# Moving the reload of the recurrence heads to GpSimd behind all Fourier columns, and spreading 32 modulation steps over 22 rounds

## Chip, cores and metric

The kernel runs on one core of a Trainium2 chip. The metric is the time of one execution on the device, in microseconds (us), as the median of several runs. The engines are named as the profile names them: PE is TensorE (matrix products; PEld is its loading of weights), DVE is VectorE, ACT is ScalarE, POOL is GpSimd, SP is SyncE, which here only issues DMAs.

## What is computed

One layer of a hybrid backbone on 512 latent and 256 context tokens of width 2048, all in float32:

```python
mod_lat = einsum("bd,ldm->lbm", silu(c), w_ada) + b_ada[:, None, :]      # six modulations
h_lat = modulate(rms_norm(x, g[0]), ml[0], ml[1])
y_lat, y_ctx = mixing_sublayer(h_lat, h_ctx, w_in, w_four, conv_w, conv_b, lru_w, lru_b, lru_lam, w_out, ...)
x = x + ml[2] * rms_norm(y_lat, g[1])
f_lat = swiglu(modulate(rms_norm(x, g[2]), ml[3], ml[4]), w_ffn_in, w_ffn_out)
x = x + ml[5] * rms_norm(f_lat, g[3])
```

`mixing_sublayer` multiplies by `w_in` and splits the columns: Fourier groups (a discrete Fourier transform over grid and channels, its real part, then a linear map per group), and recurrent head groups (a convolution, gates, a forward and a backward scan, times a GeLU gate). Both are joined and multiplied by `w_out`. `swiglu` is the channel mixer with 5632 hidden channels.

## The kernel before

**Numbers in pairs.** A float32 operand is split in two parts of a reduced format, a high part (a copy or cast, on ACT or DVE) and a low part (a subtraction, on DVE); each product is three matmuls, high by high, high by low and low by high (`mm3`). In the profile wh and wl are the parts of a weight unit, fh and fl those of a Fourier column unit, mxh and mxl those of a recurrence head.

**The stream of weights.** `Stream` holds a list of units of 512 KB in the order in which the products take them. `use` hands out one unit, and calls `prep` for the units ahead of it (`la` of them); `prep` splits a unit and calls `dma` for those still further ahead (`ra` of them). Each load takes a buffer of the pool raw, in turn, and so waits for the last reader of what lay there before; all loads of the stream are issued by SP, in order.

**Fourier columns** (395 to 490 us). 16 column units of `w_in` (n = 16 to 31 in the list) are folded (fo), split (fh, fl, ext) and multiplied into the banks f and fx. Beside them run the last gates and scans of the recurrence (`lru_step`: the ACT functions sigmoid, exp and square root, the scans on DVE); finished heads are stored to rec_d in DRAM by POOL, and each of four heads is loaded again as a unit of the stream (`rec_unit`) for the output projection. Behind n = 29, 30 and 31 stands one head each, and the last head behind them; `get_rec` takes them. In this stage `open_c` also loads the tables CX, CW, SW (raw<-cw_d), CG and SG by POOL, and splits them (th, thw, tl, tlw).

**Fourier transform and after.** From F, Fx and the tables PE forms y, whose split parts Y feed z, in two passes of 60 matmuls each; the results and the four heads are the inputs of the output projection (oq), from 527 us on.

**Second product of the channel mixer** (1615 to 2111 us). Two halves of the output columns, each of 22 rounds: one unit of activations (act_d) and two of `w_ffn_out`, 48 matmuls into the banks fo. In the first half the last modulation is summed as well: 32 steps (`gstep`), each a load of 512 KB of `w_ada` (gr, by SP, L385) and a multiply-add on DVE (ga<-gr,sil,ga). `tick(KN["Q6"])` behind each round adds Q6 to an account and issues one step for each whole number. After the half, eight matmuls gr turn the two sums ga into rows.

Instructions that one engine gets run in its program order; the order is set by the code and by priorities at build time, and every wait is a semaphore.

Of the kernel before, what the change touches and what calls it, by code (L numbers as in the profile page):

```python
# [17 lines left out]
P = 128  # L18
# [4 lines left out]
NE, NO = 258, 254  # L23
DFF = 5632
EPS = 1e-6
KN = {'p2k': 1, 'lord': 0, 'lag': 3, 'cws': 0, 'xo': 'xNcxxxcx..XX.X...C......X...C.C..C.X...X', 'xd': 3, 'order': 'xxsscxssxxxxxsssccc', 'TL': 3, 'TS': 7, 'Q7': 1.75, 'nA': 8, 'nB': 5, 'nX': 9, 'nO': 7, 'nE': 4, 'laA': 1, 'raA': 6, 'laB': 1, 'raB': 3, 'laO': 1, 'raO': 4, 'Q1': 3, 'Q2': 1.0, 'Q3': 0, 'Q4': 1.0, 'Q5': 2.5, 'Q6': 4.0, 'early': 3, 'tail': 'acb0de1f2', 'steps': 27, 'shift': 1, 'l1': 2000, 'vC': 0.1, 'pA': -100, 'vO': 0.25, 'sq': 2000, 'pO': 30, 'gvC': -2000, 'pX': -100, 'pC': -30, 'gvX': -30, 'xp': 300, 'pG': -800, 'p1': 100, 'tb': -30, 'gp': 2000, 'gvB': -30, 'vF': 0.25, 'hcp': -2000, 'mc': 800, 'rp': -800, 'vA': 0.25, 'gvF': -300, 'T2': 800, 'fs': 300, 'T5': -100, 'gvD': -100, 'op': -30, 'hp': 30, 'ni': 300, 'vB': 0.25, 'ysp': 300, 'T4': 800, 'gvR': 300, 'T1': -30, 'fi': 300, 'gvA': 800, 'T3': -800, 'pD': 800}

C_BADA, C_C, C_NG, C_CW, C_CB, C_LAM, C_LB, C_END = 0, 96, 128, 192, 224, 232, 248, 280

# [62 lines left out]
class Stream:  # L92
# [11 lines left out]
        self.lim = self.ends.popleft()  # L104
        self.prep(self.nu + self.la)

    def add(self, dmas, f):
        self.items.append([dmas, f, None])

    def dma(self, upto):  # L110
        while self.nd < min(upto, self.lim):
            it = self.items[self.nd]
            it[2] = self.alloc([1024], name="raw")
            for dst, src in it[0]:
                self.nc.sync.dma_start(dst(it[2]), src)
            self.nd += 1

    def prep(self, upto):
# [18 lines left out]
def block_kernel(ctx, tc, a, out, dump=None):  # L137
    nc = tc.nc
# [4 lines left out]
    def open_pools(side, *specs):  # L143
        stack = ExitStack()
        for n, names in specs:
            first = names.split()[0]
            cnt[0] += 1
            po = stack.enter_context(tc.tile_pool(name=f"{first}_pool{cnt[0]}", bufs=n, side=side, reuse_waits="tile"))
            for x in names.split():
                pools[x] = po  # L150
        return stack
# [5 lines left out]
    sc = open_pools("left", (8, "x ch clo"))  # L157
    sp_ = open_pools("right", (KN["nA"], RAW), (16 - KN["nA"], WH), (6, "c cT"))
    pst = ExitStack()
# [35 lines left out]
    def prq(key):  # L195
        return tc.high_priority(offset=KN.get(key, 0))

# [10 lines left out]
    def split(src, hi, lo):  # L208
        share[0] += KN.get("v" + S.key, 0)
        on_v = share[0] >= 1  # L210
        share[0] -= on_v
        (V.tensor_copy if on_v or load.even and load.t["A"] > load.t["V"] + 3000 else A.copy)(hi, src)
        V.tensor_tensor(lo, src, f(hi), op=OP.subtract)
# [31 lines left out]
        if not fill:  # L245
            owed[0] = 0.0

# [1 line left out]
    S = Stream(nc, st)  # L249
    S.pr, S.key = prq, "A"  # L250
    act_d = dr.tile([DFF, SEQ], F32, name="act_d")
# [1 line left out]
    rec_d = dr.tile([1024, SEQ], F32, name="rec_d")  # L253
# [5 lines left out]
    def kv(n):  # L259
        return lambda raw: raw.rearrange("p (k c) -> p k c", k=n)  # L260

    def wunit(w, r0, nk, c0, nw, po=("wh", "wl")):
        S.add([(kv(nk), w[r0:r0 + nk * P, c0:c0 + nw].rearrange("(k p) c -> p k c", p=P))], split_to((nk, nw), *po))
# [34 lines left out]
    def first_steps():  # L298
        g = 0
        for s in range(72):  # L300
            yield s, range(g, 64) if s == 71 else range(g, max(g, min(64, s - 7 - KN["lag"])))
            g = max(g, min(64, s - 7 - KN["lag"]))

    for s, go in first_steps():
        if s == KN["cws"]:
            S.add([(lambda raw: raw[:, 0:512].rearrange("p (k c) -> p k c", k=2), a["t_cc"].rearrange("(k p) c -> p k c", p=P))],
# [7 lines left out]
        if s < 64:  # L314
            cb, m, kq = s // 8, s // 4 % 2, s % 4
# [11 lines left out]
    def lru_w(h, d, m):  # L327
        S.add([(lambda raw, g=g: raw[:, g * 256:(g + 1) * 256].rearrange("p (k c) -> p k c", k=2),
                a["lru_w"][d, g, h, :, m * P:(m + 1) * P].rearrange("(k p) c -> p k c", p=P)) for g in range(2)], lru_prep)
# [4 lines left out]
        return hi, lo  # L334

    def rec_unit(h):
        S.add([(kv(2), rec_d[h * 256:(h + 1) * 256, :].rearrange("(k p) c -> p k c", p=P))], mix_prep)

    LRU_STEPS = [min(32, max(0, n - KN["shift"]) * 32 // KN["steps"]) for n in range(33)]
    for n in range(32):  # L340
        for c in range(LRU_STEPS[n], LRU_STEPS[n + 1]):
            if c % 4 < 2:
                lru_w(c // 8, c // 4 % 2, c % 4)
        k = n % 8
        if n < 16:
            wunit(wi, k * 256, 2, 2048 + n // 8 * 512, 512)
        else:
            c0 = (n // 8 - 2) * 512
            S.add([(kv(2), wi[k * 256:(k + 1) * 256, c0:c0 + 512].rearrange("(k p) c -> p k c", p=P))], fold_w)
            if n >= 29:  # L350
                rec_unit(n - 29)
    rec_unit(3)
    OUT = [(2, k) for k in (4, 5, 6, 7, 0, 1, 2, 3)] + [(q, k) for q in (3, 0, 1, 0, 1) for k in range(8)]
    for qd, kq in OUT:
        wunit(wo, kq * 256, 2, qd * 512, 512)
# [19 lines left out]
                wunit(a["w_ffn_out"], k * P, 1, hf * 1024, 1024, po[1 + k % 2])  # L375
    S.end()

# [1 line left out]
    gacc, graw, gmods = {}, {}, [(m, k, h) for m in (3, 4, 2, 5) for h in range(2) for k in range(KT)]  # L379

    def gload(i):
# [39 lines left out]
            T.matmul(b[:, 2 * j:2 * j + 2], acc[:, j * P:(j + 1) * P], ones[:, 0:2], start=j == 0, stop=j == 7, skip_group_check=True)  # L421
        V.tensor_copy(m34[:, m - 3, h * 8:(h + 1) * 8], b[:, 0:16].rearrange("p (j s) -> p j s", s=2)[:, :, 0])

# [1 line left out]
    xt = [[st([1024], name="x") for _ in range(2)] for _ in range(4)]  # L425
    ct = [[st([1024], name="c") for _ in range(2)] for _ in range(2)]
    st1, st2, st3 = st([P], name="stg"), st([P], name="stg"), st([P], name="stg")
# [9 lines left out]
    for z in KN["order"]:  # L437
        if z == "s":
            S.dma(S.nd + 1)
        elif z == "c":  # L440
            t, h = cts.popleft()
            nc.sync.dma_start(ct[t][h], a["ctx"][t * P:(t + 1) * P, h * 1024:(h + 1) * 1024])
        else:
            t, h = xts.popleft()
            nc.sync.dma_start(xt[t][h], a["x"][t * P:(t + 1) * P, h * 1024:(h + 1) * 1024])
    S.phase()
    while cts:
        t, h = cts.popleft()
# [16 lines left out]
    for g in (64, 96):  # L465
        V.tensor_tensor(sel, sel, ident[:, g:g + 2], op=OP.add)

# [1 line left out]
    nstat = [0]  # L469

    def rstd_of(ss, n, scale=1.0):
# [32 lines left out]
    squares(xt, 0)  # L504
    norm_in(xt, 0, 0.5)

# [1 line left out]
    S.la, S.ra = KN["laA"], KN["raA"]  # L508
    @prio("cw")
    def cw_part(row, cs):  # L510
# [26 lines left out]

    cch = ccl = cex = w4 = None

# [1 line left out]
    def xT_bank(tiles, k, o):  # L541
        for t in range(len(tiles)):
            T.transpose(o[:, t * P:(t + 1) * P], tiles[t][k // 8][:, (k % 8) * P:(k % 8 + 1) * P], ident)
# [39 lines left out]
                xT_bank(ct, 4 * kq + 2 * k + j, b[:, n * 512 + j * 256:n * 512 + (j + 1) * 256])  # L583
        A.copy(flat(cT[kq][:, 2 * ks[0]:2 * ks[-1] + 2, :]), b[:, 0:512 * len(ks)])

# [1 line left out]
    mods = cst.tile([P, 4, KT], F32, name="mods")  # L587
    hl, hc = {}, {}

# [111 lines left out]
    S.phase()  # L701
    load.even = False

# [1 line left out]
    lam = cols[:, C_LAM:C_LAM + 16]  # L705
    lt = cst.tile([P, 6, 16], F32, name="lt")
    mx, e, w, w2, acc, spc = (lt[:, i, :] for i in range(6))
# [12 lines left out]
    V.tensor_tensor(acc, acc, mx, op=OP.add)  # L720
    V.tensor_scalar(spc, acc, -8.0, None, op0=OP.mult)

# [1 line left out]
    def unfold(dst, E, O, neg=False):  # L724
        p, m = (OP.subtract, OP.add) if neg else (OP.add, OP.subtract)
        d3 = dst.rearrange("p (r c) -> p r c", c=64)
# [73 lines left out]
    S.key = "G"  # L800
    r_done(1, rb, rc)

# [1 line left out]
    sqrt_ins = []  # L804

    def lru():
# [99 lines left out]
            tick(KN["Q2"])  # L906
        g_done(grp, gb)

# [1 line left out]
    F, mix, tables = [], {}, {}  # L910
    load_c = []

    def get_rec(h):
        r = S.use()
        for m in range(2):
            mix[8 + 2 * h + m] = [tuple(x[:, m, t * P:(t + 1) * P] for x in r) for t in range(4)]
# [20 lines left out]
    for hf in range(2):  # L937
        fb = bank("f")
        for kq in range(8):
            lru_step(16 + 8 * hf + kq)  # L940
            hi, lo, ex = S.use()
            for k in range(2):
                kt = 2 * kq + k
                h = hl[kt]
                for g in range(2):
                    for e, sl in ((0, slice(0, NE)), (1, slice(NE, 512))):
                        mm3(fb[:, g * 512:(g + 1) * 512][:, sl], (hi[:, k, g, e, :], lo[:, k, g, e, :]), (h[0][:, sl], h[1][:, sl]),
                            kt == 0 and e == 0, kt == 15)
                for n in range(2):
                    T.matmul(fxb[:, 0:NE], ex[:, k, :], h[n][:, 0:NE], start=hf + kt + n == 0, stop=hf * kt * n == 15)  # L950
            if hf and kq == 4:
                open_c()
            if hf and kq > 4:
                get_rec(kq - 5)
            tick(KN["Q3"])
        for g in range(2):
            t = st([2, 512], F32R, "F")
            with prq("fs"):
                split(fb[:, g * 512:(g + 1) * 512], t[:, 0, :], t[:, 1, :])
            F.append(t)  # L960
# [2 lines left out]
    Fx = st([2, 258], F32R, "Fx")  # L963
    with prq("fs"):
        split(fxb[0:8, 0:NE], Fx[0:8, 0, :], Fx[0:8, 1, :])
    get_rec(3)

# [1 line left out]
    CX, CW, SW, CG, SG = (tables[n] for n in ("CX", "CW", "SW", "CG", "SG"))  # L969
    for pr in range(2):  # L970
        Y = []
# [41 lines left out]
            mix[c] = [(t[:, 0, i * P:(i + 1) * P], t[:, 1, i * P:(i + 1) * P]) for i in range(4)]  # L1013
    del Y, CW, SW, CX, CG, SG, F, Fx, tables

# [1 line left out]
    def out_kts(bankof, kq, ts, start, stop):  # L1017
        hi, lo = S.use()
        for t in ts:
# [27 lines left out]

    S.key = "D"

# [1 line left out]
    xr, hv, hq = {}, {}, {}  # L1051

    def p0(t):
# [71 lines left out]
                V.tensor_tensor(y[t][1], y[t][1], G2[1], op=OP.mult)  # L1125
    mix.clear()

    # ---- channel mixer, first product: seven products of half blocks (Strassen, Winograd's form), halves of gate
    # and up channels, of the contraction and of the tokens ----
    def ff_mm(o, W, nm, start):  # L1130
        for i in range(2):
            for k in range(4):
# [118 lines left out]
    ctx.enter_context(open_pools("right", (KN["nO"], RAW), (17 - KN["nO"], WH)))  # L1251
    fill.extend([gstep(i) for i in range(96, 128)])

# [1 line left out]
    S.la, S.ra, S.key = KN["laO"], KN["raO"], "O"  # L1255
    S.phase()
    y = [[None, None] for _ in range(4)]
    for hf in range(2):
# [29 lines left out]
        else:  # L1288
# [8 lines left out]
            for t in range(4):  # L1297
                y[t][1] = st([1024], name="y2")
                halves = [(0, 512), (512, 1024)] if t == 3 else [(0, 1024)]
# [5 lines left out]
                r = rstd_of(ss, 1)  # L1305
# [25 lines left out]
```

## Time and profile before

| what | us |
|---|---|
| median of 3 runs | 2120.04 (2118.46 to 2121.45) |
| span of the profiled execution | 2121.2 |
| PE busy | 2033.0 (96%) |
| DVE busy | 1457.1 (69%) |
| ACT busy | 878.3 (41%) |
| POOL busy | 81.6 (4%) |
| mean granted clock of PE, as a share of full speed | 0.982 |

The profile is of one execution, and its times count from its first instruction. The span is 1.2 us above the median. A view of the chain follows the work that ended last back to its start: each row is a stretch of time and what it was spent on. A view of waits sums the idle time before an engine's instructions by what released them. A timeline lists the instructions of one engine; the idle time before one and what ended it stand in brackets at its end. A row of windows gives the busy time of each engine in a stretch, and the clock that PE was granted there: 1.00 is 2.4 GHz, 0.50 is 1.2 GHz.

### The profile page before, as it was taken

To read this page: it belongs to the slowest core of one execution; us is meant where nothing else is said; L and a number is where in the kernel's file an instruction comes from. 1 tells how busy PE (TensorE), PEld (TensorE's weight loads), DVE (VectorE), ACT (ScalarE), POOL (GpSimd) and SP (SyncE) were. 2 spreads that over 40 slices of the span, in tenths; PEclk is the share of its full clock that TensorE was granted. 3 is DMA by queue.
4 is the path that set the end of the run, shared out by engine and by line. 5 is a ranking of instruction groups with operands and counts; after the bars stand their busy time and mean duration, and the time that the engine had idled before them with its cause. 6 is when DMAs were issued, how large, how long until landed. Compare 5 with 4: busy or idle time off the path is not lost.

```text
span 2121.2 us, 32681 instructions
## 1 busy us (share of the span) xinstructions
PE 2033.0 (96%) x13313; PEld 1821.1 (86%) x13313; DVE 1457.1 (69%) x1821; ACT 878.3 (41%) x1060; POOL 81.6 (4%) x161
## 2 busy tenths in 40 slices
PE   6999899978999979999999999999999999999998
PEld 4778787877877879999999999999998778888886
DVE  5447788997887899767777777777775753353345
ACT  6222387783235754444444444444442122132221
POOL 0000000100000000000000000000000000000000
PEclk9999999997999989999999999999999999999999
DMA  9996667534986655433433434334326964444453
GB/s 354 307 300 208 202 215 242 177 108 151 368 336 219 218 157 181 126 104 126 127 106 123 128 107 129 121 107 125 126 74 228 307 239 149 148 133 143 142 200 128
DMA packets 228998, 381.17 MB, mean 180 GB/s; under 512 B 12909, under 2 KB 151685, under 8 KB 228848
## 3 DMA queue, kind: packets, MB, share of 16 engines
q1 hardware_dynamic: 217664, 341.09, 48.5%
q0 software_dynamic: 10496, 37.33, 4.8%
q8 instruction: 104, 1.70, 0.3%
q10 hardware_dynamic: 688, 0.67, 0.1%
q14 instruction: 46, 0.38, 0.1%
HBM read 350.70 MB, written 28.34 MB: 179 GB/s over the span
## 4 chain that ended last, share of the span: by engine, by line
PE 83%; DVE 5%; DMA 4%; ACT 3%; issue 2%; POOL 0%; SPq 0%; DVEq 0%; ACTq 0%; POOLq 0%
PE xz L85 24%; PE fo L85 21%; PE fy L85 17%; PE oq L85 8%; PE r L85 4%; DMA gr<-in_w_ada 2%; PE rc L85 2%; PE ga L85 2%; PE g L85 1%; PE ada L85 1%; DVE wl L85 1%; DVE ga L85 1%; PE z L85 1%; ACT L85 1%; DVE q L85 1%
## 5 line engine op out<-in xcount | busy, mean ns | idle before, releaser
L85 DVE TENSOR_TENSOR wl<-raw,wh 128x1024 fp32r<-128x1024 f32 x219 | 264.9, 1222 | 229.2 <-ACT wh L85 188.2
L85 ACT CAST wh<-raw 128x1024 fp32r<-128x1024 f32 (+1 forms) x196 | 197.7, 1022 | 525.7 <-PE fo L85 350.6
L85 PE MATMUL fy<-h2h,wh 128*128 128x256 f32 x3024 | 371.8, 282 | 7.3 <-ACT wh L85 6.8
L85 PEld LDWEIGHTS fy<-h2h,wh 128*128 128x128 f32 x3024 | 365.3, 189 | 8.0 <-ACT wh L85 7.1
L85 PE MATMUL xz<-hq,wh 128*128 128x256 f32 x2640 | 324.0, 281 | 0.0
L85 PEld LDWEIGHTS xz<-hq,wh 128*128 128x128 f32 x2640 | 317.8, 189 | 0.0
L85 ACT CAST wh<-wr 128x1024 fp32r<-128x1024 f32 x164 | 172.4, 1053 | 252.0 <-PE fy L85 128.2
L85 PE MATMUL fo<-wh,wh 128*128 128x512 f32 x688 | 269.0, 392 | 0.2 <-DVE fe L85 0.2
L85 PE MATMUL fo<-wl,wh 128*128 128x512 f32 x664 | 260.0, 392 | 7.8 <-DVE wl L85 7.8
L85 PE MATMUL fo<-wh,wl 128*128 128x512 f32 x672 | 262.6, 391 | 0.0
L85 DVE TENSOR_TENSOR wh<-wr,wh 128x1024 fp32r<-128x1024 f32 x164 | 199.4, 1222 | 81.8 <-ACT wh L85 81.4
L85 ACT CAST wh<-ws 128x1024 fp32r<-128x1024 f32 x132 | 138.6, 1050 | 215.3 <-PE xz L85 136.0
L85 PE MATMUL xz<-h2h,wh 128*128 128x256 f32 x1632 | 213.8, 282 | 4.7 <-ACT hv L85 4.7
L85 PEld LDWEIGHTS xz<-h2h,wh 128*128 128x128 f32 x1632 | 205.1, 190 | 5.0 <-ACT hv L85 4.9
L85 DVE TENSOR_TENSOR wh<-ws,wh 128x1024 fp32r<-128x1024 f32 x132 | 161.3, 1223 | 55.7 <-ACT wh L85 55.7
L85 DVE SCALAR_TENSOR_TENSOR ga<-gr,sil,ga 128x1024 f32<-128x1024 f32 x128 | 163.8, 1281 | 49.2 <-DMA gr<-in_w_ada 48.0
L85 PEld LDWEIGHTS fo<-wl,wh 128*128 128x128 f32 x664 | 125.4, 189 | 35.8 <-DVE wl L85 9.5
L85 PEld LDWEIGHTS fo<-wh,wh 128*128 128x128 f32 x688 | 129.8, 189 | 27.8 <-DVE fe L85 0.6
L85 PEld LDWEIGHTS fo<-wh,wl 128*128 128x128 f32 x672 | 126.8, 189 | 26.5
L85 PE MATMUL ga<-uh,wh 128*128 128x512 f32 (+1 forms) x256 | 70.4, 354 | 16.9 <-ACT th L85 10.4
L85 PE MATMUL oq<-wh,mz 128*128 128x512 f32 x256 | 82.3, 398 | 0.0
L85 DVE TENSOR_TENSOR ws<-wr,wr 128x1024 f32<-128x1024 f32 x44 | 53.9, 1225 | 41.1 <-DMA wr<-in_w_ffn_in 41.1
(268 smaller groups left out, 2840.6 us busy)
## 6 DMA issues: line engine op xcount, KB each, us to landing
wr<-in_w_ffn_in SPq DMA_DIRECT2D x176, 512.0 KB, 3.6
gr<-in_w_ada SPq DMA_DIRECT2D x128, 512.0 KB, 5.9
raw<-in_w_ffn_out SPq DMA_DIRECT2D x88, 512.0 KB, 4.4
raw<-in_w_ada SPq DMA_DIRECT2D x64, 512.0 KB, 7.9
raw<-in_w_in SPq DMA_DIRECT2D x48, 512.0 KB, 4.8
raw<-in_w_out SPq DMA_DIRECT2D x48, 512.0 KB, 5.2
raw<-act_d SPq DMA_DIRECT2D x44, 512.0 KB, 3.7
act_d<-fe POOLq DMA_DIRECT2D x44, 256.0 KB, 3.3
```

The lines of the kernel that those rows point to most:

```text
L85: ins = fn(out, *args, **kw)
```

## The change

First, Q6 is 1.5 in place of 4.0. With 4 steps behind each round the 32 steps are issued in the first 8 rounds of the half; with 1.5, one and two by turns, in 22. Second, a unit of the stream can name the engine that issues its load; the recurrence heads name GpSimd, and all four now stand behind the last Fourier column unit, in the list and where `get_rec` takes them. All else that the diff removes is comments.

```diff
-'Q5': 2.5, 'Q6': 4.0, 'early': 3,
+'Q5': 2.5, 'Q6': 1.5, 'early': 3,
...
-    def add(self, dmas, f):
-        self.items.append([dmas, f, None])
+    def add(self, dmas, f, eng=None):
+        self.items.append([dmas, f, None, eng or self.nc.sync])
...
             for dst, src in it[0]:
-                self.nc.sync.dma_start(dst(it[2]), src)
+                it[3].dma_start(dst(it[2]), src)
...
     def rec_unit(h):
-        S.add([(kv(2), rec_d[h * 256:(h + 1) * 256, :].rearrange("(k p) c -> p k c", p=P))], mix_prep)
+        S.add([(kv(2), rec_d[h * 256:(h + 1) * 256, :].rearrange("(k p) c -> p k c", p=P))], mix_prep, nc.gpsimd)
...
             S.add([(kv(2), wi[k * 256:(k + 1) * 256, c0:c0 + 512].rearrange("(k p) c -> p k c", p=P))], fold_w)
-            if n >= 29:
-                rec_unit(n - 29)
-    rec_unit(3)
+    for h in range(4):
+        rec_unit(h)
...
             if hf and kq == 4:
                 open_c()
-            if hf and kq > 4:
-                get_rec(kq - 5)
...
-    get_rec(3)
+    for h in range(4):
+        get_rec(h)
```

The loads at the end of the Fourier columns, in the program order of SP, before:

```order
L115 DMA raw_4105<-in_w_in 128x2x512
L115 DMA raw_4152<-rec_d 128x2x512
L115 DMA raw_4222<-in_w_in 128x2x512
L115 DMA raw_4264<-rec_d 128x2x512
L115 DMA raw_4342<-in_w_in 128x2x512
L115 DMA raw_4384<-rec_d 128x2x512
L115 DMA raw_4390<-rec_d 128x2x512
L115 DMA raw_4432<-in_w_out 128x2x512
```

and now:

```order
L115 DMA raw_4105<-in_w_in 128x2x512
L115 DMA raw_4152<-in_w_in 128x2x512
L115 DMA raw_4222<-in_w_in 128x2x512
L115 DMA raw_4469<-in_w_out 128x2x512
L115 DMA raw_4475<-in_w_out 128x2x512
```

The two columns behind raw_4105 (n = 30 and 31) now take the buffers that head 0 and column n = 30 took. The heads' loads are in POOL's order, here from the store of a head's first half on (cw_d, t_cg and t_sg are the tables, in_b_ada belongs to a modulation):

```order
L115 DMA raw600_4264<-rec_d_86 128x2x512
L928 DMA raw605_4308<-cw_d_89 8x1024
L928 DMA raw608_4314<-cw_d_89 128x1024
L395 MEMSET ga706_4902 128x1024
L928 DMA raw611_4320<-cw_d_89 128x1024
L396 DMA ga706_4902<-in_b_ada 1x16x64
L928 DMA raw614_4326<-in_t_cg 86x774
L928 DMA raw617_4332<-in_t_sg 128x508
L115 DMA raw623_4350<-rec_d_86 128x2x512
L115 DMA raw627_4392<-rec_d_86 128x2x512
L824 DMA rec_d_86<-q552_3902 128x512
L824 DMA rec_d_86<-q553_3904 128x512
```

Behind the last store (q553) follows the load of the last head. The same place in ACT's order, before, from the last but three table loads to the last square root (th<-ga is a sigmoid, q<-q a square root, a an exponential):

```order
L85 ACT_TABLE_LOAD
L85 ACTIVATE th572_4053<-ga570_4027,cols_165 128x768
L85 ACTIVATE th573_4054<-ga571_4028,cols_165 128x768
L85 ACT_TABLE_LOAD
L85 ACTIVATE q552_3902<-q552_3902 128x768
L85 CAST ext224_1529<-raw596_4222 128x2x2
L85 CAST fh594_4214<-fo593_4210 128x4x128
L85 ACTIVATE q553_3904<-q553_3904 128x768
L85 ACT_TABLE_LOAD
L85 ACTIVATE th582_4133<-ga580_4107,cols_165 128x768
L85 ACTIVATE th583_4134<-ga581_4108,cols_165 128x768
```

and now:

```order
L85 CAST ext224_1529<-raw596_4222 128x2x2
L85 ACT_TABLE_LOAD
L85 ACTIVATE th572_4053<-ga570_4027,cols_165 128x768
L85 ACT_TABLE_LOAD
L85 ACTIVATE q552_3902<-q552_3902 128x768
L85 ACT_TABLE_LOAD
L85 ACTIVATE th573_4054<-ga571_4028,cols_165 128x768
L85 CAST fh594_4214<-fo593_4210 128x4x128
L85 ACT_TABLE_LOAD
L85 ACTIVATE q553_3904<-q553_3904 128x768
L85 ACT_TABLE_LOAD
L85 ACTIVATE th582_4133<-ga580_4107,cols_165 128x768
```

One square root now stands between two sigmoids, with a table load on each side. In DVE's order two rounds of the second product's first half read as follows now; before, such a round past the eighth held no multiply-add, and each of the first eight held four:

```order
L85 TENSOR_TENSOR wl_17369<-raw_17267,wh_17368 128x1024
L85 CAST wh_17374<-raw_17300 128x1024
L85 TENSOR_TENSOR wl_17375<-raw_17300,wh_17374 128x1024
L85 SCALAR_TENSOR_TENSOR ga_16936<-gr_17434,sil,ga_16936 128x1024
L85 TENSOR_TENSOR wl_17405<-raw_17306,wh_17404 128x1024
L85 TENSOR_TENSOR wl_17438<-raw_17336,wh_17437 128x1024
L85 TENSOR_TENSOR wl_17444<-raw_17372,wh_17443 128x1024
L85 SCALAR_TENSOR_TENSOR ga_16936<-gr_17503,sil,ga_16936 128x1024
L85 SCALAR_TENSOR_TENSOR ga_16936<-gr_17506,sil,ga_16936 128x1024
```

The multiply-adds stand between the subtractions, one or two behind every third of them.

## Rows read from the trace of the kernel before

**Rows 1.** Waits of PE, 1605 to 1870: total us, times, longest us
```profile
PE fo L85 <- DVE wl L85: 7.8, 4, 3.1
```

**Rows 2.** The chain in the second product: start us, us, what
```profile
1618.52 21.17 PE fo L85 x92
...
1664.91 23.24 PE fo L85 x94
...
1713.46 153.77 PE fo L85 x671
...
1870.67 240.03 PE fo L85 x1056
```

**Rows 3.** DVE's timeline there: start us, us, operation, [idle before <- releaser]
```profile
1662.44 1.28 DVE L85 SCALAR_TENSOR_TENSOR ga<-gr,sil,ga 128x1024 f32<-128x1024 f32 x1 [3.72 <-DMA gr<-in_w_ada]
1663.64 1.22 DVE L85 TENSOR_TENSOR wl<-raw,wh 128x1024 fp32r<-128x1024 f32 x1
1664.78 2.60 DVE L85 SCALAR_TENSOR_TENSOR ga<-gr,sil,ga 128x1024 f32<-128x1024 f32 x2
```

**Rows 4.** Windows there: us, busy by PE, PEld, DVE, ACT, POOL, PEclk, DMA share, GB/s
```profile
1620.00:1660.00 40.00, 39.08 (x172) 32.02 (x171) 27.83 (x25) 8.22 (x8) 0.00 (x0) 1.00 0.89 308
1666.00:1668.00 2.00, 2.00 (x6) 1.52 (x6) 1.97 (x3) 0.00 (x0) 0.00 (x0) 0.50 0.95 349
```

**Rows 5.** PE's timeline at the end of the Fourier columns
```profile
481.92 0.58 PE L85 MATMUL fx<-hh,ext 128*128 128x258 f32 x1 [11.85 <-DVE ext L85]
```

**Rows 6.** SP's timeline there: the last two column loads
```profile
446.01 0.37 SPq L115 DMA_DIRECT2D raw<-in_w_in  x1
...
477.30 0.37 SPq L115 DMA_DIRECT2D raw<-in_w_in  x1
```

**Rows 7.** DVE's timeline there
```profile
476.07 1.20 DVE L85 TENSOR_TENSOR mxl<-raw,mxh 128x1024 fp32r<-128x1024 f32 x1
...
479.52 1.29 DVE L85 TENSOR_TENSOR q<-q,gl 128x512 f32<-128x512 f32 x2
481.03 0.17 DVE L85 COPY fo<-raw 128x4 f32<-128x4 f32 x1 [0.22 <-DMA raw<-in_w_in]
```

**Rows 8.** ACT's timeline there
```profile
452.07 1.28 ACT L85 ACT_TABLE_LOAD   x1
453.37 0.85 ACT L85 ACTIVATE q<-q 128x768 f32<-128x768 f32 x1
...
467.64 1.58 ACT L85 ACTIVATE q<-q 128x768 f32<-128x768 f32 x2
...
489.88 1.05 ACT L85 CAST mxh<-raw 128x1024 fp32r<-128x1024 f32 x1 [3.52 <-DMA raw<-rec_d]
```

**Rows 9.** POOL's timeline there: one table's load
```profile
466.46 0.54 POOL L929 DMA_DIRECT2D raw<-cw_d  x1 [1.01 <-DVE fl L85]
```

**Rows 10.** DMAs that write or read rec_d (eight stores, four loads)
```profile
DMA to landing us min/median/max: 2.3/3.6/7.3
```

**Rows 11.** The chain in the two passes of z
```profile
501.76 10.02 PE z L85 x60
...
518.35 7.15 PE z L85 x60
```

**Rows 12.** Windows there, columns as in rows 4
```profile
461.00:470.00 9.00, 8.99 (x72) 8.46 (x70) 8.39 (x12) 8.94 (x11) 1.10 (x2) 1.00 0.34 117
474.00:491.00 17.00, 6.95 (x29) 6.38 (x29) 14.68 (x22) 4.64 (x7) 3.36 (x5) 0.50 0.61 197
498.00:508.00 10.00, 9.17 (x43) 9.17 (x44) 3.95 (x7) 2.97 (x5) 0.00 (x0) 0.50 0.29 107
```

**Rows 13.** The page's DMA issues: count, KB each, median us to landing
```profile
raw<-in_w_ffn_out SPq DMA_DIRECT2D x88, 512.0 KB, 4.4
raw<-in_w_ada SPq DMA_DIRECT2D x64, 512.0 KB, 7.9
```

**Rows 14.** The loads gr of the second product, 1615 to 1720
```profile
DMA to landing us min/median/max: 3.3/6.1/8.9
```

More of the change, by code (lines that the diff above doesn't have):

```diff
@@ L25 @@
 EPS = 1e-6
-KN = {'p2k': 1, 'lord': 0, 'lag': 3, 'cws': 0, 'xo': 'xNcxxxcx..XX.X...C......X...C.C..C.X...X', 'xd': 3, 'order': 'xxsscxssxxxxxsssccc', 'TL': 3, 'TS': 7, 'Q7': 1.75, 'nA': 8, 'nB': 5, 'nX': 9, 'nO': 7, 'nE': 4, 'laA': 1, 'raA': 6, 'laB': 1, 'raB': 3, 'laO': 1, 'raO': 4, 'Q1': 3, 'Q2': 1.0, 'Q3': 0, 'Q4': 1.0, 'Q5': 2.5, 'Q6': 4.0, 'early': 3, 'tail': 'acb0de1f2', 'steps': 27, 'shift': 1, 'l1': 2000, 'vC': 0.1, 'pA': -100, 'vO': 0.25, 'sq': 2000, 'pO': 30, 'gvC': -2000, 'pX': -100, 'pC': -30, 'gvX': -30, 'xp': 300, 'pG': -800, 'p1': 100, 'tb': -30, 'gp': 2000, 'gvB': -30, 'vF': 0.25, 'hcp': -2000, 'mc': 800, 'rp': -800, 'vA': 0.25, 'gvF': -300, 'T2': 800, 'fs': 300, 'T5': -100, 'gvD': -100, 'op': -30, 'hp': 30, 'ni': 300, 'vB': 0.25, 'ysp': 300, 'T4': 800, 'gvR': 300, 'T1': -30, 'fi': 300, 'gvA': 800, 'T3': -800, 'pD': 800}
+KN = {'p2k': 1, 'lord': 0, 'lag': 3, 'cws': 0, 'xo': 'xNcxxxcx..XX.X...C......X...C.C..C.X...X', 'xd': 3, 'order': 'xxsscxssxxxxxsssccc', 'TL': 3, 'TS': 7, 'Q7': 1.75, 'nA': 8, 'nB': 5, 'nX': 9, 'nO': 7, 'nE': 4, 'laA': 1, 'raA': 6, 'laB': 1, 'raB': 3, 'laO': 1, 'raO': 4, 'Q1': 3, 'Q2': 1.0, 'Q3': 0, 'Q4': 1.0, 'Q5': 2.5, 'Q6': 1.5, 'early': 3, 'tail': 'acb0de1f2', 'steps': 27, 'shift': 1, 'l1': 2000, 'vC': 0.1, 'pA': -100, 'vO': 0.25, 'sq': 2000, 'pO': 30, 'gvC': -2000, 'pX': -100, 'pC': -30, 'gvX': -30, 'xp': 300, 'pG': -800, 'p1': 100, 'tb': -30, 'gp': 2000, 'gvB': -30, 'vF': 0.25, 'hcp': -2000, 'mc': 800, 'rp': -800, 'vA': 0.25, 'gvF': -300, 'T2': 800, 'fs': 300, 'T5': -100, 'gvD': -100, 'op': -30, 'hp': 30, 'ni': 300, 'vB': 0.25, 'ysp': 300, 'T4': 800, 'gvR': 300, 'T1': -30, 'fi': 300, 'gvA': 800, 'T3': -800, 'pD': 800}
 C_BADA, C_C, C_NG, C_CW, C_CB, C_LAM, C_LB, C_END = 0, 96, 128, 192, 224, 232, 248, 280
```

## The prediction

> **What bounds the kernel now.** I read the busy times first: TensorE (PE) is busy for 2033.0 of 2121.2 us, so a change pays only where PE stands idle or runs at the lower of its two clock levels. I looked for both, by waits, windows, the chain and the timelines, in the two places that the diff touches.
>
> In the second product, the waits of PE in its first half name one releaser, the subtraction wl on VectorE (DVE), four times [rows 1]. The chain shows what it costs [rows 2]: the first half runs from 1618.52 to 1867.23 us, 248.7 us; the second half does the same 1056 matmuls in 240.03 us without a break, 0.227 us each, 10.9 us for a round of 48. The difference is 8.7 us, and 9.6 with the four matmuls of the first half that stand before 1618.52. Nearly all of it lies ahead of 1713.46; after that 671 matmuls run in one piece, 0.229 us each. The DVE rows show the mechanism [rows 3]: the multiply-add ga<-gr at 1662.44 has waited 3.72 us for its load to land, and the next wl stands behind that in DVE's order until 1663.64. PE starts again at 1664.91. The windows [rows 4] show DMA at 308 GB/s while 32 gr loads are crammed into eight rounds, and after a wait a stretch at granted clock 0.50, the 1.2 GHz level.
>
> At the end of the Fourier columns PE's largest wait is 11.9 us, for ext of the last column unit [rows 5]. SP's row shows why [rows 6]: that unit's load is issued only at 477.30, 31 us after the one before, and DVE's rows name what it stood for [rows 7]: it needs the buffer of recurrence head 0, which the subtraction mxl at 476.07 to 477.27 frees, far down DVE's order among scans and tables. The load lands at 481.03, where DVE's copy waits for it. But this stall is not free to take away: [rows 8 to 11] show another chain beside it, from ACT through the scans to the head stores, the reload of the last head and the Y casts, and only after these does the long product z begin at 501.76.
>
> **Part 1: 32 steps in 22 rounds.** Nothing is added or removed: 32 loads of 512 KB and 32 multiply-adds stay. A round now holds 1.5 steps in place of 4, so 4.5 loads of 0.5 MB in 10.9 us, about 216 GB/s, in place of 7 loads, 337 GB/s, which the queue did not reach. Does DVE keep up? From start to start a multiply-add takes 1.20 us, a wl 1.14 [rows 3]; a cast of the same tile is counted like a wl. Two rounds hold 6 wl, 3 multiply-adds and 1.5 casts: 6.8 + 3.6 + 1.7 = 12.1 us of 21.8. The waits for gr come on top. By the order, a gr load waits for a wl that frees its buffer, and its multiply-add stands one or two instructions behind that same wl. With L for the time from issue to landing, two rounds lose (L - 1.1) + (L - 2.3). So DVE needs 8.7 + 2L, which fits in 21.8 while L is under 6.5 us. The w_ffn_out loads, of equal size and mostly outside the crowd, took 4.4 (median) [rows 13]; gr in the crowd took 3.3 to 8.9, median 6.1 [rows 14]. I take L between the two, near 5, as a round holds 2.5 loads fewer: 18.7 of 21.8 us, and PE isn't held. The buffers for wl hold five units, so a wait of 4 us is bridged by work of PE already prepared (5.45 us a unit). The last multiply-add now stands right behind the last wl of the half, which may run while PE still has three units, 16 us, to do; so the products gr that follow the half are not late. The second half, and its end, are unchanged. **B = -9.6 us** (ends: -11, if the early rounds also gain at their start; 0, if the waits only spread; above zero under rival 3).
>
> **Part 2: heads behind the columns, on GpSimd.** The last two columns move up: the order gives n = 30 the buffer that head 0 had, n = 31 the one that n = 30 had, whose load was issued at 446.01 [rows 6]. All Fourier loads have then landed by 450, and PE can go from its last column product at about 470 straight through the rest of n = 31. That rest is 28 matmuls at 0.125 us each (72 in 9.0 us [rows 12]), 3.5 us, so it ends near 474. The 11.9 us wait is gone. What is late next? On ACT the order now has the square root of one gate alone between two sigmoid steps: two more ACT_TABLE_LOADs, 1.30 us each to the next start [rows 8], so 2.6; three casts of 512 a partition for the last columns before the last square root, each a little over half of the 1.05 of a 1024 cast, 1.8; a 1024 cast, 1.0; and ext waits about 1 us for its landing. Together some 6 us: the last square root ends near 475 in place of 469.2. All that follows it on DVE moves with it: the head product of 479.52 [rows 7] ends near 487 in place of 480.8. Then the store of the last head, now by the same GpSimd queue (issue 0.54 us [rows 9], landing 3.6 median for stores and loads of rec_d, 2.3 to 7.3 [rows 10]), to 491; the reload behind it, 0.5 and some 4, to 495.5, where before this head was cast at 489.88 [rows 8]. By the order this cast and two of w_out precede the second Y on ACT, and its subtraction precedes the first Y on DVE: Y and z start 1 us later, at about 502.8. The 11.9 us are thus turned into a wait elsewhere: +1. On the other side stands the clock. PE fell to 0.50 from 474 to 491 and again from 498 to 508 [rows 12], the second time with 60 z matmuls in 10.02 us against 7.15 for the next 60 [rows 11]. With F done, the y products from about 490 find no column work between them. Before, PE resumed at 481.9 and was at full clock by 491, 9 us later; if that holds, full clock is back at 499 to 500, and the first z costs 7.15: -2.9. The w_out loads no longer stand behind the reloads on SP. **A = +1 - 2.9 = -2 us** (ends: -15 if nothing of the new chain is late, 11.9 + 2.9; +6 if store and reload take the slow row, 3.7 + 1 more, and the clock stays low, 2.9 more).
>
> The page on ScalarE of the Trainium skill (ScalarE: Activation LUTs, "What ACT_TABLE_LOAD costs") speaks against this order: it charges each switch of the set 1.28 us for the load and 1.38 more for a drain. The trace agrees with the load alone, since the next ACTIVATE starts 1.30 us after it began; by the page's 2.66 the two switches would be 5.3 us and A would be about +1, an estimate by that page.
>
> **Sum.** Profiled execution: 2121.2 - 9.6 - 2 = 2109.6. The span is 1.2 above the median of the runs, 2120.04, so I forecast **2108.4 us**.
>
> **Rivals.**
> 1. The whole stall goes. If ACT and DVE absorb the added 6 us (parts of them wait for PE and loads anyway) and the head reload isn't on the way to z, A is 11.9 + 2.9 = -15: about 2095.5. For it: the row of PE's longest wait [rows 5]. Against: the order puts the last head's cast ahead of Y, and that head can't be stored before the scans end.
> 2. The waits for gr spread and stay. If PE has few units in hand when each load is late, the 9.6 us come back in small pieces; A alone: 2120.04 - 2 = 2118. For it: the same DVE order, wl behind a waiting multiply-add, in every round. Against: 3 us of slack in two rounds, and 671 matmuls in a piece where nothing was loaded beside w_ffn_out and act.
> 3. The slower side: gr's landing sets the pace of 22 rounds. Above L = 6.5 each further us costs 2 us in two rounds, 22 us over the half. With A at -2 the kernel is slower than before by more than the measurement's 0.2% (4.2 us) from L = 7.2, where the half loses 15.8. At the 7.9 us that loads of the same tensor took earlier [rows 13] the half loses 31 us: 2121.2 - 9.6 - 2 + 31 - 1.2 = 2139. For it: single landings of up to 8.9 [rows 14]. Against: these came with four gr loads at once.
> 4. The move doesn't do what it says: the reloads, in order on GpSimd behind tables that wait for DVE, hold the w_out casts as long as the stall did. A = 0: 2110.4. For it: GpSimd's queue does wait for DVE before each table. Beside it stands the Trainium skill (SBUF — State Buffer, "SBUF: two separate sides"): while DVE runs a copy that takes both ports, GpSimd can't write descriptors for its DMAs. GpSimd's issue took 0.54 us here [rows 9] in a stretch with DVE 8.4 of 9.0 us busy [rows 12], so the trace shows no such hold so far.
>
> **How the numbers follow.** Forecast 0.58, rival 1 0.14, rival 2 0.12, rival 3 0.07, rival 4 0.09. The forecast's own range is 2103 to 2114. To leave out no more than 2 in 10 I go down to 2099, which takes part of rival 1 in, and up to 2117, near rival 2. A measurement of this kernel tells 0.2% (4.2 us) from no change: faster by more holds for the forecast and rivals 1 and 4, 0.81; within 0.2% is rival 2, 0.12; slower is rival 3, 0.07.
>
> **What will show it.** Part 1: in the first half's chain one piece of PE from the first wl to the end, about 239 us; no row PE fo <- DVE wl but the one at the start; DMA near 216 GB/s throughout; DVE's waits for gr more in number, not in what PE waits. Part 2: no row fx <- ext; the last column load issued near 446; PE idle from about 474 to 490; last square root near 475, last head landing near 495.5; z at 502 to 504, its first 60 matmuls near 7.2 us. I am wrong in A if z starts before 497 or after 506, and in B if PE's waits for wl there sum to over 3 us.

## The result, and the profile after

| | before | after |
|---|---|---|
| median of 10 runs, us | 2120.62 (2112.60 to 2132.35) | 2106.70 (2102.67 to 2116.29) |
| profiled span, us | 2121.2 | 2104.6 |

The ratio is 0.995, with a 95% interval of 0.9926 to 0.9974; the two medians alone give 0.9934, inside it. The forecast was 2108.4, in a range of 2099 to 2117. The number came out well; one of its two terms did not, and the profile shows a third difference that nothing in the change explains. The span of 16.6 us less is made of four pieces, each read from the chains of both kernels:

| stretch | before | after | difference |
|---|---|---|---|
| start to the output projection oq | 527.18 | 530.10 | +2.9 |
| oq to the end of the gate and up product | 1088.2 | 1078.5 | -9.7 |
| from there to the second half of the second product | 255.3 | 245.3 | -10.0 |
| second half and end | 250.5 | 250.7 | +0.2 |

**The second product.** The chain after (start us, us, what) answers to [rows 2]:

```profile
1611.69 238.75 PE fo L85 x1052
1850.44 3.43 PE gr L85 x8
1853.87 240.03 PE fo L85 x1056
```

One piece from the first wl to the end of the half: 238.75 us for 1052 matmuls, the pace of the second half, as the prediction had it. PE's waits there (total us, times, longest) keep only the one at the start [rows 1]:

```profile
PE fo L85 <- DVE wl L85: 1.8, 1, 1.8
```

DVE's own waits for gr did not go. Off PE's path they grew, from 27.3 us in 8 waits before to 86.0 in 26, while its waits for ACT fell from 72.0 us to 18.5:

```profile
DVE ga L85 <- DMA gr<-in_w_ada: 86.0, 26, 5.1
DVE wl L85 <- ACT wh L85: 18.5, 11, 3.4
```

and its timeline shows a pair of rounds, with wl right behind the multiply-adds that waited [rows 3]:

```profile
1731.84 2.61 DVE L85 SCALAR_TENSOR_TENSOR ga<-gr,sil,ga 128x1024 f32<-128x1024 f32 x2 [4.40 <-DMA gr<-in_w_ada]
1734.37 0.69 DVE L85 CAST wh<-raw 128x1024 fp32r<-128x1024 f32 x1
1735.09 3.50 DVE L85 TENSOR_TENSOR wl<-raw,wh 128x1024 fp32r<-128x1024 f32 x3
1743.68 1.28 DVE L85 SCALAR_TENSOR_TENSOR ga<-gr,sil,ga 128x1024 f32<-128x1024 f32 x1 [5.09 <-DMA gr<-in_w_ada]
```

The loads gr still took 5.7 us at the median [rows 14], where 5 was assumed:

```profile
DMA to landing us min/median/max: 3.5/5.7/8.7
```

86 us of waiting in 238.75 is 7.9 in two rounds of 21.8 (the prediction's 2L - 3.4 gives 8.0 with L at 5.7), and with 12.1 us of work that is 20 of 21.8: it fits, with less to spare than the 3 us forecast. DMA moved 220 to 227 GB/s from 1640 to 1840 us (216 forecast).

**The Fourier end.** The wait for ext is gone from PE's waits between 400 and 530 us; another has taken its place, of nearly the same size [rows 5]:

```profile
PE y L85 <- ACT th L85: 11.2, 1, 11.2
...
PE y L85 <- DVE tl L85: 2.5, 1, 2.5
PE z L85 <- DVE Y L85: 1.2, 1, 1.2
```

ACT's timeline names what stands ahead of the table's cast th and then of the Y casts [rows 8]:

```profile
475.16 1.58 ACT L85 ACTIVATE q<-q 128x768 f32<-128x768 f32 x2
...
483.72 0.59 ACT L85 CAST F<-f 128x512 fp32r<-128x512 f32 x1 [5.56 <-DVE F L85]
484.20 1.05 ACT L85 CAST mxh<-raw 128x1024 fp32r<-128x1024 f32 x1
486.16 1.04 ACT L85 CAST mxh<-raw 128x1024 fp32r<-128x1024 f32 x1 [0.91 <-DMA raw<-rec_d]
487.11 0.36 ACT L85 CAST Fx<-fx 8x258 fp32r<-8x258 f32 x1
487.38 1.04 ACT L85 CAST th<-raw 8x1024 fp32r<-8x1024 f32 x1
...
498.53 1.05 ACT L85 CAST mxh<-raw 128x1024 fp32r<-128x1024 f32 x1 [2.77 <-DMA raw<-rec_d]
...
501.38 0.58 ACT L85 CAST Y<-y 86x512 fp32r<-86x512 f32 x1
```

The last square root ends at 476.7 (475 forecast). F's second cast waits for DVE, which is among the scans until then:

```profile
481.82 1.28 DVE L85 TENSOR_TENSOR_SCAN q<-th,q,th 128x512 f32<-128x512 f32 x1
483.02 0.67 DVE L85 TENSOR_TENSOR F<-f,F 128x512 fp32r<-128x512 f32 x1
```

Two heads are cast ahead of th, and the last head, landed at 498.5 (495.5 forecast), stands ahead of Y. GpSimd issued its reload in time, 0.6 us after the store had landed, and SP, no longer held by it, had begun with the w_out loads before:

```profile
492.19 0.72 POOL L115 DMA_DIRECT2D raw<-rec_d  x1 [2.33 <-DMA rec_d<-q]
...
490.17 13.93 SPq L115 DMA_DIRECT2D raw<-in_w_out  x8
```

The reload landed 6.3 us after its issue, with five w_out loads beside it, two of them issued ahead of it; that these made it slow is argued here, not shown. And the clock did not come back as forecast. The windows after (columns as in [rows 4]) against [rows 12], and the chain against [rows 11]:

```profile
491.00:501.00 10.00, 9.36 (x31) 6.29 (x32) 5.83 (x8) 4.03 (x5) 0.72 (x1) 0.50 0.89 308
501.00:511.00 10.00, 8.84 (x40) 8.31 (x40) 5.09 (x7) 3.35 (x6) 0.00 (x0) 0.50 0.51 168
511.00:521.00 10.00, 10.00 (x69) 8.10 (x69) 8.63 (x32) 5.23 (x11) 0.00 (x0) 1.00 0.00 0
```

```profile
504.35 10.36 PE z L85 x60
...
521.28 7.13 PE z L85 x60
...
530.10 15.05 PE oq L85 x64
```

PE went on at 488.5 and stayed at 0.50 until 511; the first pass of z took 10.36 us, no less than before.

**The piece that no step explains.** The gate and up product runs the same instructions without a wait in both kernels, at full granted clock. These are windows of before and of after, the same 100 us:

```profile
1000.00:1100.00 100.00, 100.00 (x845) 100.00 (x845) 76.42 (x72) 43.03 (x48) 4.28 (x6) 1.00 0.41 127
```

```profile
1000.00:1100.00 100.00, 100.00 (x855) 100.00 (x854) 76.89 (x72) 43.94 (x48) 4.28 (x6) 1.00 0.40 131
```

845 matmuls against 855: 1.1% of a stage of 840 us, which is about the 9.7 us. Whether the change or chance set this pace was the first thing to test.

### The profile page after: what moved, and what is told of

The parts are those of the page before. It is cut to its first block, busy times and chain, and to the rows that moved or that the text cites. A ratio compares the mean times of both kernels' runs of the same rounds, so it can differ in the third digit from the quotient of the medians.

```text
span 2104.6 us, 32657 instructions
## 1 busy us (share of the span) xinstructions
PE 2022.1 (96%) x13313; PEld 1810.4 (86%) x13313; DVE 1456.6 (69%) x1820; ACT 881.4 (42%) x1063; POOL 84.5 (4%) x165
## 4 chain that ended last, share of the span: by engine, by line
PE 84%; DVE 6%; DMA 5%; ACT 3%; issue 2%; POOL 0%; DVEq 0%; ACTq 0%; POOLq 0%; SPq 0%
PE xz L85 23%; PE fo L85 23%; PE fy L85 16%; PE oq L85 9%; PE r L85 4%; PE rc L85 2%; PE ada L85 2%; PE ga L85 1%; DMA gr<-in_w_ada 1%; PE g L85 1%; DVE q L85 1%; PE z L85 1%; DVE ga L85 1%; DVE wl L85 1%; ACT L85 1%
```

## The experiments

Each ratio is to runs of the kernel before that were made beside it. Times of one profile are compared by stage, from a place that all kernels share: the matmul ga at which PE goes on near 433 us (the third column counts from there to the start of z, the fourth to oq). The fifth is the first half of the second product from its first wl to gr. Paces are matmuls in 100 us of the gate and up product.

| kernel | ratio to before (95%) | to z | to oq | half | pace |
|---|---|---|---|---|---|
| before | 1 | 68.4 | 94.0 | 248.7 | 845 |
| after | 0.995 (0.9926 to 0.9974) | 71.1 | 96.9 | 238.8 | 855 |
| same kernel as before | 1.0011 (0.9988 to 1.0034) | 68.5 | 92.6 | 247.4 | 845 |
| Q6 alone | 0.9971 (0.9949 to 0.9992) | 69.2 | 92.3 | 241.2 | 845 |
| heads alone | 1.0019 (0.9994 to 1.0044) | 70.7 | 95.0 | 248.2 | 836 |
| heads by SP, Q6 1.5 | 0.9956 (0.9932 to 0.998) | 70.1 | 92.9 | 238.8 | 845 |
| after again | 0.9983 (0.9959 to 1.0008) | 71.2 | 95.5 | 238.8 | 845 |
| last head late | 1.0022 (1.0001 to 1.0043) | 74.4 | 97.7 | 246.0 | 845 |
| heads between | 0.9934 (0.9908 to 0.9959) | 66.9 | 91.3 | 238.8 | 855 |
| heads between, by SP | 0.9935 (0.991 to 0.9959) | 67.8 | 92.3 | 240.4 | 855 |

**The same kernel.** No edit.

> The kernel before, unchanged, as a kernel of its own. Between the two profiles 9.7 us vanished in the long gate and up product (775 to 1609 us), whose instructions are the same: 845 matmuls in 100 us before, 854 after, at full granted clock both times. Theory 1 (the pace differs from execution to execution, whatever the kernel): the ratio to the kernel before is 1.000 within its interval, and this profile's pace is not tied to 845. Theory 2 (the change set the pace): this profile shows 845 again, and so do all kernels without the change.

Ratio 1.0011, and 845 again, which alone decides nothing. The runs say more: the 35 runs of before spread over 2108.3 to 2131.2, 12 of them between 2108.3 and 2113.5, 21 around 2120 and two above 2130, and the 12 of this kernel spread alike. That these groups are paces is argued, not shown, since only the profiled run of each kernel shows its pace.

**Q6 alone.**

```diff
-'Q6': 4.0
+'Q6': 1.5
```

> Q6 = 1.5 alone; heads as before. Both theories: from the first wl of the second product to the gr products 238.8 us in one piece, 9.9 us less than before; PE's wait for ext stays at 11.9 us and the output projection starts at 527.2. Time: -10 us, 2110 (0.995). If spreading the steps were worth what the whole change was measured at, the other part is worth nothing. Theory 2 with the heads' move as the cause of the pace: 845 matmuls in 100 us here.

The half took 241.2 us, 7.5 less than before, not 9.9, and 6.2 less than the 247.4 of the same kernel's second profile. DVE waited longer for gr than after, in all and at the longest:

```profile
DVE ga L85 <- DMA gr<-in_w_ada: 109.7, 28, 6.6
```

The program orders differ there. Of the 32 gr loads, five are held here by the very instruction ahead of their own multiply-add, so that DVE waits for a whole landing; after, all 32 have at least one instruction between. Which unit's high part DVE also casts is carried over from earlier stages, and with the heads' move it falls on other units. So 2.4 us of the gain came only with both parts together; that the five loads are the cause is read from the orders and from a later run, and was not tried by itself. This is rival 2 in small.

**The heads alone.** The kernel after with Q6 back at 4.0 (the edit above, reversed).

> The heads' move alone, Q6 = 4.0. The forecast had -2 us for it. By the trace after it is a loss of 2.9 us (output projection at 530.1 in place of 527.2), so time +3 us, 2123; the second product's first half again takes 248.7 us from its first wl, with four waits of PE for wl. Theory 2: pace 854 here, and with it -7 us, 2113.

oq at 95.0, where the three profiles without the move have 94.0, 92.6 and 92.3: a loss, as the trace after had it, and the half again 248.2 with four waits. The pace was neither 845 nor 855 but a third, which cost this profile some 10 us (span 2129.7):

```profile
1000.00:1100.00 100.00, 100.00 (x836) 100.00 (x834) 74.76 (x70) 42.00 (x47) 3.56 (x5) 1.00 0.39 121
```

**The heads behind the columns, but by SP.**

```diff
-        S.add([(kv(2), rec_d[...])], mix_prep, nc.gpsimd)
+        S.add([(kv(2), rec_d[...])], mix_prep)
```

> As after, but the heads' loads behind the columns are issued by SP, not GpSimd. It tells whether GpSimd's queue costs anything: in the trace after, GpSimd started the last head's load 0.6 us after the store had landed and it took 6.3 us, where SP's loads of heads took 3.5 to 4.5. If the queue counts, the last head lands 2 us earlier and the output projection starts near 528; but the w_out loads stand behind it on SP again and their casts, two of which precede the second Y, come some 3 us later. I expect these to cancel: 530 to 531, and the time of after within 2 us (0.995).

I expected the two effects to cancel; oq came at 92.9, 2 to 4 us earlier than by GpSimd and no later than without the move. SP's issues of the last reload and of w_out, and the last head's cast on ACT:

```profile
489.01 0.36 SPq L115 DMA_DIRECT2D raw<-rec_d  x1
489.48 10.13 SPq L115 DMA_DIRECT2D raw<-in_w_out  x7
...
492.85 1.04 ACT L85 CAST mxh<-raw 128x1024 fp32r<-128x1024 f32 x1 [7.76 <-DMA raw<-rec_d]
...
498.19 0.57 ACT L85 CAST Y<-y 86x512 fp32r<-86x512 f32 x1
```

The cast is 62.0 us after the shared place, against 65.3 after. The reload took about 3.8 us in place of 6.3, with three w_out loads issued right behind it and none ahead; both times DMA was near full (0.98 of the share from 491 to 501 here, 0.89 after), so what differs is the order of issue and the issuing engine, and no run parts the two. z starts only 0.6 to 1.1 earlier, as w_out's casts are late in turn; the rest of the difference is the clock (first pass of z 7.44 us in this execution, as with Q6 alone). So moving the queue to GpSimd brought nothing here.

**After again.** No edit.

> The changed kernel once more. So far the profiles show three paces in the unchanged gate and up product: 835 (heads alone), 845 (four kernels) and 854 matmuls in 100 us (after), some 9.8 us apart over that stage, and the runs of the kernel before fall in three groups near 2110, 2120 and 2130. Theory 1 (the pace is drawn anew in each execution): the runs of this kernel fall in groups 10 us apart again, and the pace of this profile may be any of the three. Theory 2 (the pace belongs to the kernel's build): 854 again and runs in one group. Stages of the change: Fourier end +2 to +3 us, second product -10: ratio 0.9965.

```profile
1000.00:1100.00 100.00, 100.00 (x845) 100.00 (x844) 76.42 (x71) 43.16 (x48) 4.28 (x6) 1.00 0.41 128
```

The kernel that ran at 855 runs at 845 here, and its runs spread over 2103.5 to 2125.6. So theory 2 fails: the build does not fix the pace. Theory 1 fits, with one thing open. The first four experiments ran on one chip (14) and the last four on another (13), and for the first profiles no chip is on record. Chip 14 showed 836 and 845, chip 13 845 and 855, so the chip alone does not fix the pace either; but no kernel was profiled at two paces on a chip known to be the same. The ratio, 0.9983, is 0.3% above the first one; with 9.8 us between paces, ten or twelve runs do not settle the last 0.2%. By stage the change is worth +2.8 (oq at 96.9, 95.5 and 95.0 against 94.0, 92.6 and 92.3, means) and -9.4 (the half at 238.8 twice against 248.7, 247.4 and 248.2), so -6.6 us, 0.9969, between the two ratios.

**The last head late.** Its unit behind three w_out units, taken before the fourth block of oq.

```diff
-    for h in range(4):
+    for h in range(3):
         rec_unit(h)
...
-    for qd, kq in OUT:
+    for n, (qd, kq) in enumerate(OUT):
+        if n == 3:
+            rec_unit(3)
...
-    for h in range(4):
+    for h in range(3):
         get_rec(h)
...
+            if qd == 2 and n == 3:
+                get_rec(3)
```

> As after, but the last head's unit stands behind the first three w_out units and is taken just before the fourth block of the output projection, so that its cast (which waited 2.8 us for the reload and stood ahead of the Y casts) is out of Y's way. From the place where PE goes on near 433 us to the start of z it took 68.6 to 69.4 us in the kernels without the move and 70.7 to 71.1 with it by GpSimd. If the last head is what z waits for: the second Y cast comes 3 us earlier, z starts 68 us after that place. Rival (w_out's casts or the tables hold Y as well): under 1 us. Time: 0.995 or 0.9965.

Missed, on the other side: z at 74.4 (68 expected). In ACT's order a w_out cast took the head's place, and ahead of Fx and th instead of behind them:

```profile
490.83 1.04 ACT L85 CAST wh<-raw 128x1024 fp32r<-128x1024 f32 x1 [5.64 <-DMA raw<-in_w_out]
491.78 0.36 ACT L85 CAST Fx<-fx 8x258 fp32r<-8x258 f32 x1
492.05 1.04 ACT L85 CAST th<-raw 8x1024 fp32r<-8x1024 f32 x1
```

So th waits for whatever load the order puts ahead of it on ACT; that confirms the place, not the price. The half lost most of Part 1's gain too, at 246.0 us: five gr loads again are held by the instruction ahead of their multiply-add, and DVE waited about as long for gr as with Q6 alone (PE more, 6.4 us at wl and wh, 2.7 of them ahead of the half's first matmul). Why the half is 4.8 us longer than with Q6 alone stays open:

```profile
DVE ga L85 <- DMA gr<-in_w_ada: 114.0, 28, 6.1
```

**The heads between the two passes of z.**

```diff
-    for h in range(4):
-        get_rec(h)
...
+        if pr == 0:
+            for h in range(4):
+                get_rec(h)
```

> As after, but all four heads are taken between the two passes of z. Then the casts of heads 1 and 2 don't stand ahead of the table CX on ACT either, for which y waits 11 us in the trace after (its cast at 487.4 could come at 484.6). Theory: z starts 2.8 + 3.4 us earlier than in after, 65 us after PE goes on near 433, and the output projection 6 us earlier, 90 to 91 us after it; ratio 0.992. Rival (the scans' end on DVE holds the tables' low parts, and the heads' casts then crowd the second pass of z): z at 69 or later, output projection no earlier, 0.9965.

z started at 66.9, 4 us earlier than after (6 expected), oq at 91.3 (90 to 91 expected). PE's long wait is 9.59 in place of 11.15:

```profile
484.08 0.72 PE L85 MATMUL y<-th,Fx 8*86 8x512 f32 x1 [9.59 <-ACT th L85]
```

What is left of it is ACT's wait for DVE at the casts of F, 5.56 us as after, which this edit does not touch: DVE is in the scans then. The half stayed at 238.8. This version and the next have the lowest ratios; by stage oq comes 4 to 5 us earlier than with the change alone, and the rest of 0.9934 fits the pace, as its profile happens to be one of 855.

**The same, by SP.** The edit of the fourth run on top.

> As the one before, but the heads' loads are issued by SP. w_out's loads then stand behind the reload of the last head, which waits for its store; the first w_out cast stands ahead of the second Y cast on ACT. With the heads behind all columns by SP (fourth run) z started 70.1 us after PE went on near 433. If GpSimd's queue was only the lesser evil: here z starts at 69 to 70, later than by GpSimd by 4 us, ratio 0.9955. If the SP queue costs nothing: as the one before, 0.992.

z at 67.8 and oq at 92.3, 1 us later than by GpSimd, not 4, and the ratio the same. (The half's 240.4 is one piece without a wait; 1609 to 1612 us ran at granted clock 0.50.) With the heads out of Y's way the queue matters little.

## Why the prediction was right, and where it was not

- Part 1, -9.6 forecast, -10.0 measured (-9.4 on the mean of the profiles). The mechanism and the size hold: four waits and two stretches at the low clock went, the half runs at the second half's pace. The room was overestimated (DVE has under 2 us of 21.8 left, 3 forecast), because gr loads kept 5.7 us. Q6 alone gave -7.5; rival 2 was real where the buffers' turn is bad.
- Part 2, -2 forecast, +2.8 measured: the sign was wrong. The steps up to the stall were right: it went, the last square root came about 7 us later (6 forecast), the head reload behind it, and z is later. The step that failed is "full clock is back at 499 to 500, and the first z costs 7.15: -2.9". It rested on one interval, 9 us, in which PE had also worked on columns. After, from 491.64 on, PE ran y products instead, 9.36 of 10.00 us busy at 0.50, and in the three profiles with the move by GpSimd full clock came 22.5, 14.0 and 13.6 us after PE went on. The first pass of z took 10.36, 8.92 and 8.92 us there, against 10.02, 8.48 and 7.44 without the move. The clock gave nothing back; on the means it cost 0.75, which makes some 3.6 of the 4.8 us by which Part 2 was off.
- The rest is the other term of Part 2, "z at about 502.8, +1", for which the prediction names two orders but works out no sum. z came at 504.35 in the first profile and 2.3 us later on the mean (71.1, 71.2, 70.7 against 68.4, 68.5, 69.2); the last head landed 3.0 us later than forecast, as its reload took 6.3 us in place of about 4. How much of z's delay this reload makes is not shown: by SP the head was cast 3.3 us earlier, and z started only 0.6 to 1.1 earlier. With all heads out of the way z started 4 us earlier.
- The page's price of a table load (the Trainium skill, ScalarE: Activation LUTs, "What ACT_TABLE_LOAD costs"), with its drain, gave A at about +1 by the estimate in the prediction; the trace after again shows the load alone and no drain: a load at 453.57, the next ACTIVATE at 454.86. A was positive for other reasons.
- Rival 1 (all of the stall gone) fell: PE waited 11.2 us for th in its place. Rival 3 did not come: gr's median landing, 5.7 us, stayed below 6.5, though single ones took up to 8.7. Rival 4 had the size of the stall right (11.2 us for 11.9), not its cause: th was held by heads' casts and by DVE, not by w_out.
- That the total came within 2 us of the forecast is luck. By stage the change is worth -6.6 us, which would have given about 2113.5, still inside the range; the two measurements say -10.6 (-15.7 to -5.5) and -3.6 (-8.7 to +1.7). The 4 us between stage and first measurement made good what Part 2 lost. They fit the pace of the executions compared, which the runs without a profile do not show.

## What to carry to other kernels

A stall that names one late load is worth only the distance to the next thing that the same engine waits for; list the order of the engine behind it (here ACT's casts) before booking it. Spread background work until each round has room, and look at whether a load is held by the instruction right ahead of its own consumer: the two kernels here that had this lost part of the gain, though it was not tried alone. And measure a change by its stage before trusting a total whose executions differ by more than the change.

## What the runs showed of the hardware

Matmuls of 256 columns with a weight load each ran, in different executions, at 836, 845 or 855 in 100 us (48 of them in 5.76, 5.70 or 5.63 us, so 0.1200, 0.1187 or 0.1173 us each), at granted clock 1.00 and without a wait, in any one execution the same from 900 to 1400 us; the same kernel showed two of the three. The 512-column matmuls of the second product took 0.2273 us in all of them. What sets the pace stays open.

GpSimd's issue of a 512 KB load took 0.72 us where SP's took 0.37. Three of its four loads of heads landed after 3.9 to 4.0 us, where SP's in the same order (fourth experiment) took 3.5 to 3.7. The fourth took 6.3 us, with two w_out loads issued ahead of it and three behind, where SP's took about 3.8 with three issued behind it and none ahead.
